# An output projection with seven products in place of eight, and the scheduler that was changed with it

## The chip, the cores and the metric

The kernel runs on all 8 cores of one Trainium2 chip. Each core computes one eighth of the tokens. The metric is the device time of the slowest core, in microseconds (us). Before the change it was 1244.42 us (median of the 3 executions, 1244.34 to 1245.89).

Each execution lists, for every core, its span and the mean clock that TensorE was granted, as a share of full speed. An execution is called slow when one die (cores 0 to 3, or 4 to 7) is over 1% longer than the other at a lower clock, or when its time is over 1.5% above the fastest of the same kernel. The rule has a gap that matters below: when two cores of each die are at a lower clock, the dies agree with each other, and the execution counts as fast unless a quicker one of the same kernel stands beside it.

In the profile PE is TensorE, PEld its weight loads, DVE VectorE, ACT ScalarE, POOL GpSimd, SP the engine that issues most transfers. A name before "<-" is what an instruction writes.

## The reference

Four sequences of 8192 tokens, 1024 wide. What the change touches is the output projection of the mixer, `w_out`, 1024 x 1024. A second part of the block, the squared-ReLU MLP, comes after it and takes over half of the time.

```python
def reference(x, ...):
    h = rmsnorm(x, norm1_g[l])
    p = jnp.einsum('bsd,de->bse', h, w_in[l])          # B, C, x~ | u, v
    ...
    y_a = b_gate * causal_depthwise_conv(c_gate * xc, conv_w[l])
    y_b = u * spatial_gating(layernorm(v, ...), gmlp_ws[l], gmlp_bs[l])
    y = jnp.concatenate([rmsnorm(y_a, out_norm_conv_g[l]),
                         rmsnorm(y_b, out_norm_gmlp_g[l])], axis=-1)
    x = x + jnp.einsum('bse,ed->bsd', y, w_out[l])     # <- the output projection
    h2 = rmsnorm(x, norm2_g[l])
    a = jax.nn.relu(jnp.einsum('bsd,df->bsf', h2, w_up[l]))
    x = x + jnp.einsum('bsf,fd->bsd', a * a, w_down[l])
    return rmsnorm(x, final_g)
```

## The kernel before

A core works on 8 tiles of 512 tokens (`MT = 512`, `NMT = 8`). The mixer goes through the tiles one after the other, until about 440 us. Then the MLP works on pairs of tiles (groups `g`). The MLP already uses a seven-product form (Strassen-Winograd) of its two large products: each operand is cut in four quarters, three sums of quarters are added to it (`[7, 4, ...]` buffers), and seven products of quarters replace eight.

The output projection is plain. Each of 8 output chunks is a sum of 8 matmuls of 128x128 weights on 512 columns:

```python
def out_proj(m):
    b = X[(m + 1) % 3]
    for dc in range(8):
        bank = bank8()
        for e0 in (0, 4):
            pe(bank, [(bank[:, :], WO[:, e_, dc * 128:(dc + 1) * 128], YN[:, e_, :], e_ == 0, e_ == 7)
                      for e_ in range(e0, e0 + 4)], YN.keys(e0, 4) + WO.keys(0, 8))
        tt(b[:, dc, :], bank[:, :], b[:, dc, :], ALU.add, bank.keys() + b.keys(dc), b.keys(dc))
        ...                                    # stores of x1, two chunks at a time
    rs = RS[nxt("rs", 3)]
    rstd(rs[:, :], stats(b, X1Q, 8, ONESD), MT, rs.keys())
    dma("sp", rs_d[m], rs[:, :], rs.keys(), [("rsd", m)], ("rss", m % 2), 4 * 128 * MT)
```

The last statement stores each tile's reciprocal deviations (`RS`) in memory, as `rs_s`. The MLP loads them again, with the stored x1, to make its input `H2` (this is `h2_part`; the table goes to `RSL`, the rows to `XS`):

```python
def h2_part(g, h):
    m, rs = 2 * g + h, RSL[h]
    dma("pool", rs[:, :], rs_d[m], [("rsd", m)], rs.keys(), ("rsl", h), 4 * 128 * MT, margin=4.0)
    for j in range(4):
        xs = XS[nxt("xs", 2)]
        ...
        dma("pool", xs[:, :, :], src, [("x1", m, j)], xs.keys(0, 2), ...)
        for k in (2 * j, 2 * j + 1):
            q = ((3, 2), (4, 1))[k // 4][h]
            stt(H2[:, q, k % 4, :], xs[:, k % 2, :], pcol(G2, k), rs[:, :], ALU.mult, ALU.mult, ...)
```

Buffers have fixed places in the core's memory. Mixer buffers and MLP buffers lie on top of each other, and a write to a place waits for the last reads of whatever lay there: `keys` gives a buffer's kilobytes, and the dependency tracking goes by them. The places that matter (KB, from `o`):

```python
VH = ar.buf("VH", (o + 98) * KB, [4, MT], F16)                                   # mixer
RS = [ar.buf(f"RS{i}", (o + 190 + 2 * i) * KB, [MT], F32) for i in range(3)]     # both
WO = ar.buf("WO", (o + 166) * KB, [8, 1024], F16)                                # mixer
YN = ar.buf("YN", (o + 182) * KB, [8, MT], F16)                                  # mixer
SN = [ar.buf(f"SN{i}", (o + a) * KB, [3, MT], F32) for i, a in enumerate((98, 104, 182))]   # MLP
RSL = [ar.buf(f"RSL{i}", (o + 196 + 2 * i) * KB, [MT], F32) for i in range(2)]   # MLP
```

The order of the instructions on each engine isn't that of the program text. A list scheduler (`S.schedule`) simulates the five engines, picks an order, improves it by some rounds that go backward from the end, and fixes it when the kernel is built.

Of the kernel before, what the change touches and what calls it, by code (L numbers as in the profile page):

```python
# [17 lines left out]
MT = 512  # L18
# [4 lines left out]
HW = 32  # L23
KB = 1024

ENGS = ("pe", "act", "dve", "pool", "sp")

# [35 lines left out]
def real(x):  # L63
    return x.ap() if isinstance(x, Late) else x


class Sched:
# [44 lines left out]
    def schedule(self, phys, rounds=8):  # L112


        base = [(op, op.deps) for op in self.ops]
        best = None
        for _ in range(rounds + 1):
            for op, deps in base:
                op.deps = deps
                for b in op.banks:  # L120
                    b.left = len(b.ops)
            order = self.place([op for op, _ in base], phys)
            est = max(o.finish for o in order)
            if best is None or est < best[0]:
                best = (est, order, [(o, o.deps) for o in order],
                        [(o.opens, o.opens.phys) for o in order if o.opens is not None],
                        {o: (o.start, o.finish) for o in order})
            self.push(order, est)
        self.est_total, self.ops = best[:2]
        for o, deps in best[2]:  # L130
            o.deps = deps
            o.start, o.finish = best[4][o]
        for b, p in best[3]:
            b.phys = p
        self.by_eng = {e: [o for o in self.ops if o.eng == e] for e in ENGS}

    def push(self, order, est, lat=0.12, dma_lat=2.0, dma_rate=290e3):
# [13 lines left out]
        def dur(o):  # L151
            return o.dur if o.dma_key is None else o.occ + o.nbytes / dma_rate + dma_lat + 2 * o.margin
        while True:
# [12 lines left out]
            if o.dma_key is not None:  # L166
                dma_free = min(dma_free, o.late - dma_lat - 2 * o.margin) - o.nbytes / dma_rate
                end = min(end, dma_free)
# [9 lines left out]
    def place(self, ops, phys, lat=0.12, dma_lat=2.0, dma_rate=290e3):  # L178
# [13 lines left out]
        dma_free = 0.0  # L192
        cold = 3.4
        order = []
        while True:
            best = None
            for e in ENGS:
# [5 lines left out]
                def ready_at(o):  # L203
                    return o.ready_t if o.opens is None else max(o.ready_t, soon)
# [10 lines left out]
            if op.opens is not None:  # L215
                f = min(free, key=lambda f: f[1])
                free.remove(f)
                op.opens.phys = f[0]
                op.deps = op.deps + f[2]
# [10 lines left out]
            if op.dma_key is not None:  # L230
                dma_free = max(dma_free, st + op.occ) + op.nbytes / dma_rate
                op.finish = dma_free + dma_lat + op.margin
            else:
                op.finish = st + op.dur - op.occ + occ
# [11 lines left out]
        assert len(order) == len(ops)  # L246
# [73 lines left out]
def build_program():  # L320
# [23 lines left out]
    with es:  # L344
# [23 lines left out]
        SQ = [ar.buf(f"SQ{i}", (o + 68 + 4 * i) * KB, [4, MT], BF16) for i in range(2)]  # L368
        HT = [ar.buf("HT0", (o + 126) * KB, [8, MT], F16), ar.buf("HT1", (o + 76) * KB, [8, MT], F16)]
        PREP = [ar.buf(f"PREP{i}", (o + 84 + 7 * i) * KB, [7, 4, 128], F16) for i in range(2)]  # L370
        VH = ar.buf("VH", (o + 98) * KB, [4, MT], F16)
        CT = [ar.buf(f"CT{i}", (o + 102 + 2 * i) * KB, [MT], F32) for i in range(2)]
        T2 = [ar.buf(f"T2{i}", (o + 106 + 2 * i) * KB, [MT], F32) for i in range(2)]
        X = [ar.buf(f"X{i}", (o + a) * KB, [8, MT], F32) for i, a in enumerate((134, 110, 150))]
        WO = ar.buf("WO", (o + 166) * KB, [8, 1024], F16)
        YN = ar.buf("YN", (o + 182) * KB, [8, MT], F16)
        RS = [ar.buf(f"RS{i}", (o + 190 + 2 * i) * KB, [MT], F32) for i in range(3)]
        XQ = [ar.buf("XQ0", (o + 126) * KB, [8, MT], BF16), ar.buf("XQ1", (o + 76) * KB, [8, MT], BF16)]
        X1Q = ar.buf("X1Q", (o + 182) * KB, [8, MT], BF16)
# [8 lines left out]
        RSL = [ar.buf(f"RSL{i}", (o + 196 + 2 * i) * KB, [MT], F32) for i in range(2)]  # L388
# [7 lines left out]
        HQ = [ar.buf("HQ0", (o + 106) * KB, [8, HW], BF16), ar.buf("HQ1", (o + 108) * KB, [8, HW], F16)]  # L396
        SQH, HH = HQ[0][:, :, :], HQ[1][:, :, :]
        WSB = [ar.buf(f"WSB{i}", (o + 84 + 2 * i) * KB, [MT], F32) for i in range(3)]
# [30 lines left out]
        def act(out, in_, func, reads, writes, n=MT, **kw):  # L429
            aps = sum(1 for v in kw.values() if not isinstance(v, (int, float)))  # L430
            S.add("act", lambda e: e.activation(out=out, in_=real(in_), func=func, **kw), reads=reads, writes=writes,  # L431
                  occ=(n / 1.2 + 200 + 70 * aps) / 1000, banks=[in_.bank] if isinstance(in_, Late) else [])

        def dve(fn, reads, writes, n=MT, rate=1, src=None):
            S.add("dve", fn, reads=reads, writes=writes, occ=(n / rate + 151) / 960,
                  banks=[src.bank] if isinstance(src, Late) else [])
# [71 lines left out]
        def stage0_norm(m, bank, step=4):  # L508
            rs = RS[nxt("rs", 3)]
# [38 lines left out]
        def stage_conv(m, c):  # L548
# [7 lines left out]
            ct = CT[nxt("ct", 2)]  # L556
            act(ct[:, :], bC[:, :], AF.Identity, bC.keys(), ct.keys())
            tt(Z[:, c, 128:640], bX[:, :], ct[:, :], ALU.mult, bX.keys() + ct.keys(), Z.keys(c))
# [7 lines left out]
        def stage_su(m, c):  # L566
# [7 lines left out]
            t2 = T2[nxt("t2", 2)]  # L574
            bias_b = BIAS[:, c, :].unsqueeze(1).broadcast_to([128, 4, 128])
            stt(t2[:, :].rearrange("p (t i) -> p t i", t=4), bS[:, :].rearrange("p (t i) -> p t i", t=4),
                pcol(GLN, c), bias_b, ALU.mult, ALU.add, bS.keys() + [("BIAS",)] + CONST, t2.keys())
            tt(YB[:, c, :], bU[:, :], t2[:, :], ALU.mult, bU.keys() + t2.keys(), YB.keys(c))

        def y_norm(src, q, ebase):  # L580
            rs = RS[nxt("rs", 3)]
            rstd(rs[:, :], stats(src, q, 4, ONESE), MT, rs.keys())
            for c in (0, 2):
                tt(YN[:, ebase + c:ebase + c + 2, :], src[:, c:c + 2, :],
                   rs[:, :].unsqueeze(1).broadcast_to([128, 2, MT]), ALU.mult, src.keys(c, 2) + rs.keys(),
                   YN.keys(ebase + c, 2), n=2 * MT)

        def out_proj(m):
            b = X[(m + 1) % 3]
            for dc in range(8):  # L590
                bank = bank8()
                for e0 in (0, 4):
                    pe(bank, [(bank[:, :], WO[:, e_, dc * 128:(dc + 1) * 128], YN[:, e_, :], e_ == 0, e_ == 7)
                              for e_ in range(e0, e0 + 4)], YN.keys(e0, 4) + WO.keys(0, 8))
                tt(b[:, dc, :], bank[:, :], b[:, dc, :], ALU.add, bank.keys() + b.keys(dc), b.keys(dc))
                if dc % 2:
                    j = dc // 2
                    dst = x1_d[m, :, 2 * MT * j:2 * MT * (j + 1)].rearrange("p (k t) -> p k t", k=2)
                    dma("sp", dst, b[:, 2 * j:2 * j + 2, :], b.keys(2 * j, 2), [("x1", m, j)], ("xs", (m + 1) % 3, j),
                        4 * 128 * 2 * MT)  # L600
            rs = RS[nxt("rs", 3)]
            rstd(rs[:, :], stats(b, X1Q, 8, ONESD), MT, rs.keys())
            dma("sp", rs_d[m], rs[:, :], rs.keys(), [("rsd", m)], ("rss", m % 2), 4 * 128 * MT)

        def combine(p, dst, src, dkeys, reads, margin):
# [4 lines left out]
            tt(p[:, 4, :, :], p[:, 3, :, :], p[:, 2, :, :], ALU.add, p.keys(2, 2), p.keys(4), rate=2)  # L610
            tt(p[:, 3:6:2, :, :], p[:, 0:1, :, :].broadcast_to([128, 2, 4, 128]), p[:, 3:5, :, :], ALU.subtract,
               p.keys(0) + p.keys(3, 2), p.keys(3) + p.keys(5), n=1024, rate=2)
            tt(p[:, 6, :, :], p[:, 1, :, :], p[:, 5, :, :], ALU.add, p.keys(1) + p.keys(5), p.keys(6), rate=2)
# [5 lines left out]
        def prep(i, n):  # L619
            combine(PREP[n % 2], ws(i), wup_d if i < 16 else wdn_d, (i, ("pl", n % 2), ("ps", n % 2)), WO.keys(4) if n < 2 else [], 5.0)  # L620

# [9 lines left out]
        def load_w(n):  # L631
            s, i = wslot(), plan[n]
            if n < 32 and 16 <= i < 24:
# [86 lines left out]

        def down_unit(o_, s0, s1):
            bA, bC, bD = banks_acd()

# [11 lines left out]
            d1, d2 = o_, o_ + 4  # L735
            prod(bA, P1, True, False)
            addr(0, d1, bA)
            prod(bD, P2, True, True)
            addr(0, d1, bD)
            prod(bC, P5, True, False)  # L740
            addr(1, d2, bC)
            prod(bA, P6, False, False)
            addr(1, d1, bA)
            prod(bC, P3, False, True)
            addr(1, d1, bC)
            prod(bA, P7, False, False)
            addr(1, d2, bA)
            prod(bA, P4, False, True)
            addr(0, d2, bA)

        def final(g):

            rss = []
            for h in range(2):
                b, rs = R[h], RS[nxt("rs", 3)]
# [99 lines left out]
        for j in range(2):  # L855
            wload(WO[:, 4 * j:4 * j + 4, :], wo_d[j].rearrange("p (k n) -> p k n", k=4), WO.keys(4 * j, 4), ("o", j),
                  2048 * KB)
            gain(lambda k_: WO[:, k_, :], WO, range(4 * j, 4 * j + 4), GCONV, 1024)
# [38 lines left out]
        def prep_some(m):  # L897
            if m >= 1 and pos["prep"] < 24:
                n = pos["prep"]
                prep(n if n < 16 else n + 8, n)  # L900
# [3 lines left out]
        for m in range(NMT):  # L904
# [16 lines left out]
            y_norm(YA, SQ[0], 0)  # L921
            if last:
                h2_part(0, 1)
                h2_sums()
# [144 lines left out]
```

## Time and profile before

| | before |
|---|---|
| time, median | 1244.42 us |
| spans of the 8 cores in the profiled execution | 1235.7 to 1244.9 us |
| granted clock, mean of each core | 0.991 to 0.995 |
| PE busy | 1209.6 us, 97% of the span |
| DVE busy | 893.4 us, 72% |
| output projection on PE | 512 matmuls of 512 columns |

These lines are from the page of the kernel before (core 7, the slowest): the busy times, the granted clock in 40 slices of the span in tenths, the chain of work that ended last, and the group of the output projection's matmuls (busy time, mean ns of one, idle before).

```profile
PE 1209.6 (97%) x5880; PEld 548.5 (44%) x5880; DVE 893.4 (72%) x1377; ACT 530.4 (43%) x905; POOL 86.0 (7%) x146
...
PEclk9899999999999999999999999999999999999998
...
PE 93%; DMA 5%; DVE 1%; issue 0%; SPq 0%; DVEq 0%; POOLq 0%
...
L424 PE MATMUL PS<-YN,WO 128*128 128x512 f16 x512 | 113.8, 379 | 0.0
```

PE is the chain. The mean of 379 ns is the time from a matmul's start to its end in the pipeline. What a matmul costs is the distance between starts. On core 7's PE timeline 368 matmuls of 512 columns start in the 79.43 us from 719.62 to 799.05 us, 215.8 ns apart. (The prediction took 100 us / 465 = 215.05 ns from the last line of the next view. That is a little too low: a window counts every matmul that touches it, one that began before it too.) The view is the windows of core 7, with the busy time of each engine and its instructions, the granted clock, the share of the transfer engines and GB/s.

```profile
core 7: us, PE busy (x) PEld busy (x) DVE busy (x) ACT busy (x) POOL busy (x), PEclk, DMA share, GB/s
...
100.00:400.00 300.00, 300.00 (x1534) 135.22 (x1533) 235.63 (x328) 157.08 (x268) 15.36 (x29) 1.00 0.73 199
400.00:425.00 25.00, 25.00 (x118) 11.27 (x115) 19.58 (x30) 9.56 (x15) 2.13 (x4) 1.00 0.94 305
425.00:450.00 25.00, 25.00 (x141) 11.25 (x140) 22.58 (x31) 13.49 (x22) 1.60 (x3) 1.00 0.55 180
...
660.00:760.00 100.00, 100.00 (x465) 45.31 (x464) 69.04 (x109) 37.29 (x66) 11.29 (x16) 1.00 0.72 243
```

PE has no gap in any of these windows. DVE has some slack in the mixer (235.63 of 300 us), and the least in the stretch from 425 to 450 us, where the mixer turns into the MLP (22.58 of 25). I call that stretch the turn. Why PE doesn't wait there shows in the POOL timeline of core 1, in which GpSimd issues the loads for `H2` (start, duration, what, and in brackets the idle time before and what ended it):

```profile
169.83 0.54 POOL L450 DMA_DIRECT2D RSL_100<-rs_s  x1 [3.02 <-DMA rs_s<-RS_79]
...
407.94 0.53 POOL L450 DMA_DIRECT2D XS_94<-x_s  x1 [11.21 <-DVE H_96 L442]
```

The table of tile 1's deviations (RSL_100) was asked for at 169.83 us, long before it was needed. The second half of `H2` was complete at 425.42 us (DVE timeline), and its sums began at 426.60 us. So PE had MLP matmuls (those that read H_96) to put between the last pieces of the mixer, as its timeline of core 1 shows:

```profile
430.54 1.89 PE L424 MATMUL PS<-H_96,RING_83 128*128 128x512 f16 x8
432.26 1.03 PE L424 MATMUL PS<-H_96,RING_84 128*128 128x512 f16 x4
433.12 1.89 PE L424 MATMUL PS<-H_96,RING_83 128*128 128x512 f16 x8
...
438.31 1.89 PE L424 MATMUL PS<-YN,WO 128*128 128x512 f16 x8
```

### The profile page before, as it was taken

What the parts mean: (1) busy time and instruction counts of PE and PEld (TensorE: products, weight loads), DVE (VectorE), ACT (ScalarE), POOL (GpSimd) and SP (SyncE); (2) the same over time, 40 slices, a digit from 0 to 9 for tenths busy, and PEclk for the clock granted to TensorE, in tenths of its full rate; (3) what the DMA queues carried; (4) which work ended last, traced back from release to release, by engine and by line L of the source; (5) the groups of instructions that cost most, each with busy time, mean ns of one, the idle gap of its engine ahead of it and who ended that gap; (6) DMA issues with size and microseconds to landing.
All of it is one profiled execution on the core that took longest, in us unless ns stands there. A gap on an engine that the chain in (4) does not pass through costs nothing.

```text
span 1244.9 us, 18564 instructions; the slowest of 8 cores (1235.7 to 1244.9 us)
## 1 busy us (share of the span) xinstructions
PE 1209.6 (97%) x5880; PEld 548.5 (44%) x5880; DVE 893.4 (72%) x1377; ACT 530.4 (43%) x905; POOL 86.0 (7%) x146
## 2 busy tenths in 40 slices
PE   5899999999999999999999999999999999999994
PEld 3444444444444444444444444444444444444442
DVE  2778687877878887658759737767846876855746
ACT  4544655536554356026127205317405406503524
POOL 0100000000001011000101200000110000110000
PEclk9899999999999999999999999999999999999998
DMA  8968688596675869975577764576984645985423
GB/s 185 171 148 232 167 228 231 148 245 175 179 220 153 279 213 207 237 266 176 169 260 228 262 212 162 211 237 177 295 272 148 216 165 182 279 271 177 149 90 135
DMA packets 55183, 253.81 MB, mean 204 GB/s; under 512 B 6192, under 2 KB 6320, under 8 KB 54832
## 3 DMA queue, kind: packets, MB, share of 16 engines
q1 hardware_dynamic: 35152, 180.27, 42.8%
q0 software_dynamic: 19936, 72.36, 25.3%
q8 instruction: 49, 0.80, 0.3%
q14 instruction: 46, 0.38, 0.1%
HBM read 211.71 MB, written 65.01 MB: 222 GB/s over the span
## 4 chain that ended last, share of the span: by engine, by line
PE 93%; DMA 5%; DVE 1%; issue 0%; SPq 0%; DVEq 0%; POOLq 0%
PE PS L424 93%; DMA WSB_109<-bsf 2%; DMA X_74<-xT 1%; DMA X_73<-xT 1%; DMA WV<-wv 1%; DMA WCXB_53<-wcxb 1%; DVE RA L439 0%; DVE RB L439 0%; SPq L450 0%; DVE WU L446 0%; DVEq L344 0%; DVE FSQ_102 L439 0%; DVE FSQ_101 L439 0%; DVE Z L439 0%; DVEq L284 0%
## 5 line engine op out<-in xcount | busy, mean ns | idle before, releaser
L439 DVE TENSOR_TENSOR RB<-PS,RB 128x512 f32<-128x512 f32 x128 | 87.4, 690 | 91.4 <-PE PS L424 88.9
L424 PE MATMUL PS<-YN,WO 128*128 128x512 f16 x512 | 113.8, 379 | 0.0
L439 DVE TENSOR_TENSOR RA<-PS,RA 128x512 f32<-128x512 f32 x96 | 66.1, 690 | 60.6 <-PE PS L424 59.2
L439 DVE TENSOR_TENSOR A_89<-A_89 128x512 bf16<-128x512 bf16 (+1 forms) x192 | 94.5, 508 | 8.2 <-ACT A_89 L431 3.6
L431 ACT ACTIVATE SN_92<-PS 128x512 f32<-128x512 f32 x63 | 37.4, 595 | 106.5 <-PE PS L424 104.7
L424 PEld LDWEIGHTS PS<-YN,WO 128*128 128x128 f16 x512 | 50.1, 98 | 60.4
L424 PE MATMUL PS<-A_89,RING_83 128*128 128x512 bf16 x308 | 76.1, 379 | 0.0
L424 PE MATMUL PS<-A_89,RING_85 128*128 128x512 bf16 x308 | 76.1, 379 | 0.0
L424 PE MATMUL PS<-A_89,RING_86 128*128 128x512 bf16 x308 | 75.8, 379 | 0.0
L424 PE MATMUL PS<-A_89,RING_84 128*128 128x512 bf16 x308 | 75.5, 379 | 0.0
L424 PE MATMUL PS<-H_96,RING_87 128*128 128x512 f16 x308 | 75.1, 379 | 0.0
L424 PE MATMUL PS<-H_96,RING_83 128*128 128x512 f16 x308 | 74.5, 379 | 0.0
L424 PE MATMUL PS<-H_96,RING_88 128*128 128x512 f16 x308 | 74.3, 379 | 0.0
L424 PE MATMUL PS<-H_96,RING_84 128*128 128x512 f16 x308 | 74.3, 379 | 0.0
L431 ACT ACTIVATE SN_90<-PS 128x512 f32<-128x512 f32 x66 | 39.2, 595 | 76.7 <-PE PS L424 75.6
L424 PE MATMUL PS<-A_89,RING_88 128*128 128x512 bf16 x280 | 69.4, 379 | 0.0
L424 PE MATMUL PS<-A_89,RING_87 128*128 128x512 bf16 x280 | 69.1, 379 | 0.0
L431 ACT ACTIVATE SN_93<-PS 128x512 f32<-128x512 f32 x64 | 38.2, 596 | 71.8 <-PE PS L424 71.3
L424 PE MATMUL PS<-H_96,RING_85 128*128 128x512 f16 x280 | 67.9, 379 | 0.0
L424 PE MATMUL PS<-H_96,RING_86 128*128 128x512 f16 x280 | 67.4, 379 | 0.0
L431 ACT ACTIVATE SN_91<-PS 128x512 f32<-128x512 f32 x63 | 37.5, 595 | 70.1 <-PE PS L424 68.0
L439 DVE TENSOR_TENSOR SN_92<-PS,SN_92 128x512 f32<-128x512 f32 x63 | 43.4, 690 | 27.4 <-PE PS L424 22.7
(231 smaller groups left out, 2029.2 us busy)
## 6 DMA issues: line engine op xcount, KB each, us to landing
RING_83<-ws_s SPq DMA_DIRECT2D x21, 896.0 KB, 6.0
RING_84<-ws_s SPq DMA_DIRECT2D x21, 896.0 KB, 6.4
RING_87<-ws_s SPq DMA_DIRECT2D x20, 896.0 KB, 5.3
RING_88<-ws_s SPq DMA_DIRECT2D x20, 896.0 KB, 6.2
RING_85<-ws_s SPq DMA_DIRECT2D x19, 896.0 KB, 6.0
RING_86<-ws_s SPq DMA_DIRECT2D x19, 896.0 KB, 6.3
ws_s<-PREP_65 SPq DMA_DIRECT2D x12, 896.0 KB, 6.3
ws_s<-PREP_66 SPq DMA_DIRECT2D x12, 896.0 KB, 5.6
```

Of the source, the lines that this page charges most:

```text
L424: ins = e.matmul(real(o_), lhsT=l, rhs=r, start=st, stop=sp, skip_group_check=True)
L431: S.add("act", lambda e: e.activation(out=out, in_=real(in_), func=func, **kw), reads=reads, writes=writes, occ=(n / 1.2 + 200 + 70 * aps) ...
L439: dve(lambda e: e.tensor_tensor(out=out, in0=real(in0), in1=in1, op=op), reads, writes, n, rate, in0)
```

## The change

The intent is to give the output projection the same seven-product form, so that PE has an eighth less to do there, and to schedule better. The diff has these parts:

1. `WO` and `YN` become quarters with sums, `[7, 4, ...]`. The columns of a tile are cut in two token halves, so the matmuls have 256 columns, and there are 896 of them instead of 512. DVE makes the sums of `YN` for each tile and those of `WO` once, and adds 14 PSUM results per tile instead of 8.
2. `WO` grows from 16 to 28 KB and `YN` from 8 to 14 KB, so the buffers are placed anew.
3. The scheduler models two transfer queues that share a rate, tries 60 disturbed orders, and picks the one that is best on average over 6 draws of late transfers. Its costs of ACT and DVE instructions are new too.
4. In the last tile, the second half of `H2` comes after the loop of `stage_su` in the program text, not before it.
5. Small changes go with these: two temporaries (`CT`, `T2`) are gone and their results are made in place in `Z` and `YB`, other weights of the down product are combined during the mixer, and the scheduler holds back some PSUM banks.

```diff
-        VH = ar.buf("VH", (o + 98) * KB, [4, MT], F16)
+        YN = ar.buf("YN", (o + 68) * KB, [7, 4, MT // 2], F16)
+        RS1 = [ar.buf(f"RS1{i}", (o + 104 + 2 * i) * KB, [MT], F32) for i in range(3)]
-        WO = ar.buf("WO", (o + 166) * KB, [8, 1024], F16)
-        YN = ar.buf("YN", (o + 182) * KB, [8, MT], F16)
-        RS = [ar.buf(f"RS{i}", (o + 190 + 2 * i) * KB, [MT], F32) for i in range(3)]
+        WO = ar.buf("WO", (o + 166) * KB, [7, 4, MT], F16)
+        VH = ar.buf("VH", (o + 194) * KB, [4, MT], F16)
...
-        RSL = [ar.buf(f"RSL{i}", (o + 196 + 2 * i) * KB, [MT], F32) for i in range(2)]
+        RS2 = [ar.buf(f"RS2{i}", (o + 190 + 2 * i) * KB, [MT], F32) for i in range(3)]
+        RSL = [ar.buf(f"RSL{i}", (o + 198 - 2 * i) * KB, [MT], F32) for i in range(2)]
...
         def out_proj(m):
-            for dc in range(8):
-                ...
+            x = X[(m + 1) % 3]
+            half = MT // 2
+            for dc in (0, 2):
+                def prod(bank, p, first, last):
+                    a, b = p
+                    pe(bank, [(bank[:, half * u:half * (u + 1)], WO[:, a, k, (dc + u) * 128:(dc + u + 1) * 128],
+                               YN[:, b, k, :], first and u == 0 and k == 0, last and k == 3)
+                              for u in range(2) for k in range(4)],
+                       YN.keys(b) + WO.keys(a))
+                ...
+                winograd(prod, add, dc)        # 7 products, 7 adds
+            rs = RS1[nxt("rs", 3)]
+            rstd(rs[:, :], stats(x, X1Q, 8, ONESD), MT, rs.keys())
             dma("sp", rs_d[m], rs[:, :], rs.keys(), [("rsd", m)], ("rss", m % 2), 4 * 128 * MT)
...
-            y_norm(YA, SQ[0], 0)
+            y_norm(YA, SQ[0], (3, 2))
             if last:
-                h2_part(0, 1)
-                h2_sums()
                 refill(4)
             for c in range(4):
                 stage_su(m, c)
+            if last:
+                h2_part(0, 1)
+                h2_sums()
+            y_norm(YB, SQ[1], (4, 1))
+            tsum(lambda i, j, d: YN[:, i:j:d, :, :], lambda j: YN.keys(j), 2 * MT)
...
-    def schedule(self, phys, rounds=8):
+    def schedule(self, phys, rounds=8, tries=60):
+        draws = [{op: rnd.choice((0.0, 0.0, 0.0, 1.0)) * rnd.uniform(1.0, 8.0) * (not op.fixed) for op in dmas} for _ in range(6)]
+        ...                                    # 60 disturbed orders, the best mean over the draws is kept
```

## The prediction

> **What bounds it now.** The TensorE matmul stream. The chain of waits is 93% PE, one unbroken run from 68.7 to 1227.0 us. In the windows from 100 to 1200 us PE is busy without a gap at granted clock 1.00; 100 us of the MLP hold 465 matmuls of 512 columns, 215.05 ns each. Outside that run lie 68.7 us of start (about 50 us PE busy, the rest waiting for loads) and 18 us of tail. DVE is busy 37.5 to 42 of every 50 us in the mixer windows (100 to 450 us): second, not binding.
>
> **Removed.** By the groups, the output projection is 512 matmuls of 512 columns: 512 x 0.215 = 110.1 us, all inside the unbroken run.
>
> **Added.** 7/8 of the columns, as 896 matmuls of 256 columns. The profile has none of that width. Estimate: [...] the start's burst of fifty-two 128-wide ones takes 55 ns each, each with its weight load hidden. So a 256-wide one should take 108.5 ns: 97.2 us. [...] Saving on PE: **12.9 us**.
>
> **DVE pays.** Per tile 14 instead of 8 PSUM adds (six more at 0.605 us, the start-to-start distance in the DVE timeline; their 690 ns "mean" overlaps) and about 2.3 us of half-precision sums of YN: +6 us in a tile of about 49.5 us. DVE goes from about 39 of 49.5 to about 45 of 48 us, some 93%. DVE frees the PSUM banks, so small PE stalls may appear in the mixer; I allow 1.5 us. Once, WO needs sums too (about 4.5 us of DVE near 85 to 95 us); other PE work covers them. ACT (about 26 of 50 us) has room. The MLP, over half of the time, keeps its instructions.
>
> **Start and tail.** PE loses about 19 us to waits and some 3 us to a low clock before 68.7 us, waiting for transfers (DMA share 0.82 to 1.03 up to 60 us), which the change does not shorten, only splits and reorders. One thing looks worse: in the new DVE order the gain multiplications of the fourth conv weight's (WCXB) second half and of WU's second half stand behind the BIAS add that waits for the bsf table, which landed at 66 us. If it lands as late again, PE runs dry earlier. A better model of two queues may win elsewhere. Net allowance +1.5 us, uncertain by 4. Tail unchanged within 1 us. The late-transfer part of the scheduler can win nothing in the middle: PE has no gap there.
>
> **Sum.** 1244.4 - 12.9 + 1.5 + 1.5 - 0.5 = about **1234 us** (0.8% faster), 8 in 10 between 1226.5 and 1241.5. Faster by over 2%: 0.04; within 2%: 0.94; slower by over 2%: 0.02.
>
> **What would show it.** Right: the YN,WO group becomes 896 matmuls of 128x256 spaced 108.5 ns in the timeline; DVE busy rises by 45 to 50 us, to near 940, above 44 of 50 in mixer windows; MLP windows still 465 matmuls per 100 us; the unbroken PE run about 1146 us long. Stall step: PE busy under 50 of 50 in mixer windows, released by DVE adds. Start step: where the unbroken run begins, with a PE wait on WCXB or WU gains.
>
> **What would make it wrong.** Spacing well above 108.5 ns (weight loads not hidden at 256 columns); DVE saturating in the mixer and stalling PE by more than 5 us; a start 5 us or more longer or shorter through the new order; a late transfer meeting the fixed orders; a lower granted clock.

The sum came to 1244.4 - 12.9 + 1.5 + 1.5 - 0.5 = 1234.0 us. The 108.5 ns was the estimate. The measured numbers give nearly the same: a straight line from 55 ns at 128 columns (the 52 matmuls of the start) to 215.05 ns at 512 gives 108.35 ns at 256, 97.1 us for 896 of them, and a saving of 13.0 us in place of 12.9.

## The result, and the profile after

| | before | changed |
|---|---|---|
| time, median of 4 | 1244.38 us (1243.37 to 1245.89) | 1286.27 us |
| all executions | 1244.42, 1244.34, 1245.89, 1243.37 | 1287.64, 1485.55, 1284.06, 1284.9 |
| ratio of the fast executions | | 1.0332 (1.0302 to 1.0363) |

A ratio is the mean time of one kernel's fast executions over that of the other's fast executions of the same rounds, so it isn't quite the ratio of the medians. The interval is the 95% one. The changed kernel is 3.3% slower, not 0.8% faster. In the fast executions of the changed kernel behind this ratio a pair of cores on each die was at 0.960 to 0.966, so it isn't a comparison at equal clock; the controls below are.

The lines of the page that answer to those shown of before (core 4, the slowest; its clock wasn't that of core 7 before, so the sums can't be compared directly):

```profile
PE 1230.3 (96%) x6264; PEld 594.6 (46%) x6264; DVE 942.6 (73%) x1460; ACT 531.2 (41%) x905; POOL 87.7 (7%) x148
...
PEclk9999999999999997888889999999999999999997
...
PE 91%; DMA 4%; DVE 2%; issue 1%; ACT 1%; SPq 0%; DVEq 0%; ACTq 0%
...
L496 PE MATMUL PS<-YN,WO 128*128 128x256 f16 x896 | 107.2, 276 | 5.4 <-DVE YN L512 3.1
```

The PEclk row drops to 7 and 8 tenths in slices 16 to 21 of 40. The list of cores of the same execution, with span and mean granted clock, shows on whom:

```profile
core 0: 1245.7 us, clock 0.990
core 1: 1236.9 us, clock 0.991
core 2: 1283.2 us, clock 0.963
core 3: 1279.7 us, clock 0.960
core 4: 1286.1 us, clock 0.960
core 5: 1280.7 us, clock 0.964
core 6: 1241.1 us, clock 0.990
core 7: 1246.1 us, clock 0.986
```

So there are two effects. Cores 2 to 5, at a lowered clock, took 38 to 50 us longer than in the profile before. But the cores that kept their clock (0, 1, 6, 7) didn't gain anything either: core 1 took 1236.9 us, against 1237.7 us before.

**Core 1: where the saving went.** Its PE timeline first shows that the matmuls have the predicted cost, 40 of them from 91.52 to 95.89 us, that is 109.2 ns each. Then, at the turn, it shows four waits that the kernel before had not:

```profile
91.52 4.53 PE L496 MATMUL PS<-YN,WO 128*128 128x256 f16 x40
95.89 0.59 PE L496 MATMUL PS<-HT_66,WCXB_52 128*128 128x512 f16 x2
...
398.79 0.41 PE L496 MATMUL PS<-WST,VH 128*64 128x128 f16 x8
...
429.81 5.40 PE L496 MATMUL PS<-YN,WO 128*128 128x256 f16 x48 [2.43 <-DVE YN L512]
435.87 1.91 PE L496 MATMUL PS<-YN,WO 128*128 128x256 f16 x16 [0.66 <-DVE X_76 L512]
439.49 2.78 PE L496 MATMUL PS<-YN,WO 128*128 128x256 f16 x24 [1.72 <-DVE X_76 L512]
444.75 1.02 PE L496 MATMUL PS<-H_92,RING_79 128*128 128x512 f16 x4 [2.47 <-DVE H_92 L512]
```

They sum to 7.28 us. Every core has three or four of these waits, 5.15 to 7.28 us in sum. The POOL timeline of core 1 shows what was late:

```profile
399.75 0.54 POOL L523 DMA_DIRECT2D RSL_99<-rs_s  x1 [1.43 <-ACT Z L503]
416.21 0.53 POOL L523 DMA_DIRECT2D XS_90<-x_s  x1 [15.92 <-DVE H_92 L515]
...
420.02 0.53 POOL L523 DMA_DIRECT2D XS_91<-x_s  x1
```

RSL_99 is the table that was asked for at 169.83 us before. Now it is asked for at 399.75 us, right after the last matmul that reads VH (398.79 us, the third line of the PE rows), on which it lies. The bracket names an ACT write of Z, the releaser that came last by the profile, but Z isn't on that place; the load leaves 0.55 us after the end of those matmuls (398.79 + 0.41 us), and did so on every core that was looked at. It took 12.4 us to land. The multiplications that make `H2` wait for it, they free the XS buffers late, and the last loads leave at 416 and 420 us. The second half of `H2` was complete at 441.2 us (before: 425.4). So PE had no MLP matmuls to fill the time in which DVE finishes the mixer, and stood still.

The windows of core 1 count it: PE was busy 17.73 of 25 us at the turn, with DVE at 22.81 of 25, much as before (22.03 in the same window of this core).

```profile
100.00:400.00 300.00, 299.33 (x1888) 167.65 (x1887) 275.14 (x392) 162.76 (x274) 15.60 (x30) 1.00 0.74 199
...
425.00:450.00 25.00, 17.73 (x124) 12.17 (x123) 22.81 (x31) 8.40 (x13) 3.04 (x5) 0.93 0.66 210
...
500.00:550.00 50.00, 50.00 (x234) 22.64 (x232) 19.32 (x28) 5.66 (x10) 0.55 (x1) 1.00 0.41 133
```

A further cost comes after some of these waits: a clock of half speed for a while. On core 4 the same 48 matmuls took 6.93 us where they took 5.40 us on core 1, and the granted clock was 0.50 from 431.2 to 434.4 us. The 0.93 in the second line above comes from such a stretch on core 1: after the last of its waits the granted clock was 0.70 in the mean from 444.7 to 448 us. Over 418 to 510 us, in the control below, the waits of PE are 13.0 us in the mean over 8 cores, and the half clock takes about 3.4 us more. Before, it was 0.3 us of waits and none.

**Core 4: a second wait, then the clock.** Seven of the 8 cores have another wait between 480 and 500 us, of 2.4 to 11.85 us. These are rows of core 4's timelines of SP, ACT and PE, in that order:

```profile
468.47 1.40 SPq L523 DMA_DIRECT2D rs_s<-RS_72  x1
```

```profile
496.85 0.60 ACT L503 ACTIVATE SN_87<-PS 128x512 f32<-128x512 f32 x1 [12.87 <-DMA rs_s<-RS_72]
```

```profile
497.59 1.87 PE L496 MATMUL PS<-H_92,RING_83 128*128 128x512 f16 x4 [11.85 <-ACT SN_87 L503]
```

The last tile's deviations are stored from RS_72, and the store landed 28.3 us after its issue (the three before it from that buffer took 8.1 to 11.9 us on this core), among loads of weights with the transfer engines at 0.95 of their time (the window from 485 to 490 us). The first write to that part of SN_87 that lies on RS_72 in the new places waited for it (other parts had been written at 470.94 and 471.80 us), and PE waited for a free bank.

Then the clock. The windows of core 4:

```profile
450.00:500.00 50.00, 38.09 (x171) 16.98 (x170) 28.48 (x46) 21.68 (x38) 5.59 (x8) 0.88 0.87 233
500.00:550.00 50.00, 50.00 (x188) 20.56 (x187) 21.90 (x34) 7.40 (x13) 0.00 (x0) 0.80 0.31 106
550.00:660.00 110.00, 110.00 (x421) 45.56 (x420) 69.17 (x112) 33.09 (x57) 7.98 (x15) 0.81 0.63 167
660.00:760.00 100.00, 100.00 (x463) 45.24 (x462) 78.31 (x125) 40.81 (x67) 12.87 (x19) 1.00 0.83 279
```

The granted clock was 0.50 from 490 to 502 us, during and after the wait. From about 503 to 662 us PE ran at 0.81, and did 421 matmuls in 110 us where it did 511 before (cores 3 and 7). The two cores of a pair went down and came back together: 159.5 us on both cores 4 and 5, 162.8 us on both cores 2 and 3. That is about 160 x (1 - 0.81) = 30 us of work. Then, under the same load, the clock returned to full speed: 1.00, with 463 matmuls in the 100 us from 660 us on core 4. Core 1 kept 1.00 from 500 to 760 us.

So two cores of each die were lowered and the other two were not (mean clock 0.960 to 0.964 on cores 2 to 5, 0.986 to 0.991 on the others), although PE had been busy for 409 to 422 of the 430 us from 70 to 500 us on all 8.

**A ledger.** To compare runs I use a lag: a moment t of the PE timeline, minus the columns of all matmuls that started by then, at 2.4 columns per ns (2400 per us). This is the rate at full clock by the spacings above: 256 columns more cost 215.8 - 109.2 = 106.6 ns, and 256 / 106.6 = 2.40. The mean over 8 cores, in us (the expectations below worked from sums over windows, which count some matmuls twice and give lags lower by up to 9 us):

| profiled execution | at 100 us | 420 | 510 | 1200 |
|---|---|---|---|---|
| before | 24.1 | 28.8 | 30.6 | 41.1 |
| changed, result run (pairs lowered) | 25.9 | 31.7 | 51.5 | 76.4 |
| changed, first control below (none lowered) | 25.9 | 31.7 | 50.2 | 61.7 |

About 1% of the records of two cores in each profile are missing, which raises their lag a little. The changed kernel has 32768 columns less per core (896 x 256 against 512 x 512), 13.65 us. For an execution without lowered pairs: -13.65 (columns), +1.8 (start, 25.9 - 24.1), +1.1 (mixer from 100 to 420 us, 5.8 against 4.7), +16.7 (420 to 510 us, 18.5 against 1.8), +1.0 (MLP, 11.5 against 10.5). The sum is +7.0 us; the mean span of the 8 cores rose by 6.6 us (1240.0 to 1246.6), which agrees. So the stretch from 420 to 510 us alone eats more than the saving.

### The profile page after: what moved, and what is told of

It is laid out like the page before. It is cut to its first block, busy times and chain, and to the rows that moved or that the text cites. A ratio compares the mean times of both kernels' runs of the same rounds, so it can differ in the third digit from the quotient of the medians.

```text
span 1286.1 us, 19491 instructions; the slowest of 8 cores (1236.9 to 1286.1 us)
## 1 busy us (share of the span) xinstructions
PE 1230.3 (96%) x6264; PEld 594.6 (46%) x6264; DVE 942.6 (73%) x1460; ACT 531.2 (41%) x905; POOL 87.7 (7%) x148
## 3 DMA queue, kind: packets, MB, share of 16 engines
q0 software_dynamic: 21760, 72.36, 25.9%
## 4 chain that ended last, share of the span: by engine, by line
PE 91%; DMA 4%; DVE 2%; issue 1%; ACT 1%; SPq 0%; DVEq 0%; ACTq 0%
PE PS L496 91%; DMA rs_s<-RS_72 2%; DMA X_76<-xT 1%; DMA X_75<-xT 1%; DVE RA L512 0%; DVE RB L512 0%; DVE YN L512 0%; DVE X_76 L512 0%; SPq L523 0%; DVE H_92 L512 0%; ACT XQ_68 L503 0%; ACT RS_73 L503 0%; ACT RS_71 L503 0%; ACT DUMP_56 L503 0%; DVE WCXB_54 L519 0%
## 5 line engine op out<-in xcount | busy, mean ns | idle before, releaser
L496 PE MATMUL PS<-YN,WO 128*128 128x256 f16 x896 | 107.2, 276 | 5.4 <-DVE YN L512 3.1
L496 PEld LDWEIGHTS PS<-YN,WO 128*128 128x128 f16 x896 | 88.2, 99 | 26.7 <-issue 7.4
L503 ACT ACTIVATE SN_87<-PS 128x512 f32<-128x512 f32 x63 | 37.4, 595 | 134.5 <-PE PS L496 121.5
L496 PE MATMUL PS<-H_92,RING_83 128*128 128x512 f16 x308 | 78.2, 393 | 11.9 <-ACT SN_87 L503 11.9
L496 PE MATMUL PS<-A_85,RING_81 128*128 128x512 bf16 x308 | 80.9, 395 | 0.0
L496 PE MATMUL PS<-A_85,RING_82 128*128 128x512 bf16 x308 | 80.8, 394 | 0.0
L496 PE MATMUL PS<-A_85,RING_80 128*128 128x512 bf16 x308 | 79.3, 389 | 0.0
L496 PE MATMUL PS<-A_85,RING_79 128*128 128x512 bf16 x308 | 79.3, 389 | 0.0
L496 PE MATMUL PS<-H_92,RING_79 128*128 128x512 f16 x308 | 76.7, 385 | 2.5 <-DVE H_92 L512 2.5
L496 PE MATMUL PS<-H_92,RING_80 128*128 128x512 f16 x308 | 78.1, 396 | 0.0
L496 PE MATMUL PS<-H_92,RING_84 128*128 128x512 f16 x308 | 76.7, 389 | 0.0
L503 ACT ACTIVATE SN_86<-PS 128x512 f32<-128x512 f32 x66 | 39.3, 596 | 87.3 <-PE PS L496 87.1
L496 PE MATMUL PS<-A_85,RING_83 128*128 128x512 bf16 x280 | 72.2, 388 | 0.0
L496 PE MATMUL PS<-A_85,RING_84 128*128 128x512 bf16 x280 | 71.7, 387 | 0.0
L503 ACT ACTIVATE SN_88<-PS 128x512 f32<-128x512 f32 x63 | 37.1, 594 | 82.8 <-PE PS L496 82.8
L496 PE MATMUL PS<-H_92,RING_81 128*128 128x512 f16 x280 | 70.5, 385 | 0.0
L496 PE MATMUL PS<-H_92,RING_82 128*128 128x512 f16 x280 | 70.4, 388 | 0.0
L512 DVE TENSOR_TENSOR SN_87<-PS,SN_87 128x512 f32<-128x512 f32 x63 | 43.1, 688 | 36.4 <-PE PS L496 18.2
L512 DVE TENSOR_TENSOR SN_88<-PS,SN_88 128x512 f32<-128x512 f32 x63 | 43.1, 688 | 27.4 <-PE PS L496 19.0
```

The source lines that it names most:

```text
L496: ins = e.matmul(real(o_), lhsT=l, rhs=r, start=st, stop=sp, skip_group_check=True)
L503: S.add("act", lambda e: e.activation(out=out, in_=real(in_), func=func, **kw), reads=reads, writes=writes, occ=(n / 1.2 + 70 + 70 * aps) ...
L512: dve(lambda e: e.tensor_tensor(out=out, in0=real(in0), in1=in1, op=op), reads, writes, n, rate, in0)
```

## The experiments

Theories at this point:

- The turn: the waits come from the new places (RSL on VH, SN on RS). Rivals: the new scheduler's order makes them; or VectorE simply has too much to do in the last tile.
- The clock: the waits of PE just before bring it (A); or it comes with this instruction stream whatever its waits, or with chip and moment.

Letters in the expectations below are those of the time they were written; in the second call, C is "the place of RSL" and D "VectorE is crowded"; in the calls after it, A is "the wait brings the lowered clock", B "the instruction stream", C "chip and moment". In kernels made for experiments the profile leaves out the buffer numbers of names (H for H_92, SN for SN_87).

### First call, four kernels on chip 1: before 1245.52 us, median of 7

**e0_after_again: the changed kernel, unedited.** A control on another chip.

> The changed kernel itself, again, perhaps on another chip. If the slowdown belongs to the program (a wait for the store of the last tile's rstd, then a lowered clock), it comes back here: about 1280 to 1290 us, a PE wait of 5 to 12 us near 490 us for ACT SN, and on some pairs of cores a granted clock near 0.81 for about 165 us after it. If it was a mood of that chip, this comes at about 1240 to 1250 us with a clock near 0.99 on all cores.

Measured: 1258.67, 1250.51, 1251.65 us fast, ratio 1.0063 (1.0031 to 1.0095), and one slow one, 1483.3 us, with cores 2 and 3 at 0.964 and 0.961 beside die 1 at 0.81 to 0.82. So without the lowered clock the changed kernel is 0.6% slower than before, and the 33 us more of the result run's fast executions (41 against 8 us above before) go with the clock. The waits at the turn were there on all 8 cores, the one on the rs_s store too (0.9 to 9.7 us).

**e1_rs_moved: only the last tile's deviations elsewhere.** The order of every engine is the changed kernel's (it was frozen, and compared instruction by instruction). The dependencies were worked out anew for the new place, where nothing of the first MLP steps lies.

```diff
-            rs = RS1[nxt("rs", 3)]
-            rstd(rs[:, :], stats(x, X1Q, 8, ONESD), MT, rs.keys())
-            dma("sp", rs_d[m], rs[:, :], ...)
+            at = RS2[2] if m + 1 == NMT else rs        # applied after scheduling, order kept
+            rstd(at[:, :], stats(x, X1Q, 8, ONESD), MT, rs.keys())
+            dma("sp", rs_d[m], at[:, :], ...)
```

> The changed kernel with the order of every engine frozen as it was; only the last tile's rstd is kept in a buffer that no SN tile overlaps, so that the first SN write does not wait for its store. Theory A (that wait makes PE idle for 9 to 12 us, and the idle stretch is what lowers the clock of a pair of cores afterwards): the wait is gone, no window below 0.97 clock between 500 and 680 us, all cores 1228 to 1240 us, time about 1236 to 1240 us. Rival B (the clock is lowered by the heavier load of the new mixer, or by the 7 us of waits at 426 to 447 us, and the store wait is a bystander): the store wait is gone, but some cores still show 0.81 for over 100 us, and the time stays above 1265 us.

Measured: 1250.38, 1243.22, 1254.82, 1250.9 us, ratio 1.0033 (0.9997 to 1.0069). The wait for SN is gone from all cores, which shows its cause. The mean lag at 510 us fell from 50.2 to 43.8 us. The time expected (1236 to 1240 us) was missed. Some cores wait instead for a weight load that used to hide behind that wait, core 3 for instance:

```profile
497.72 2.72 PE L524 MATMUL PS<-A,RING 128*128 128x512 bf16 x6 [4.37 <-DMA RING<-ws_s]
```

The waits of 7 us at the turn stay. No execution had a lowered pair.

**e2_before_stalls: the kernel before, made to wait.** Its order is frozen, and 23, 13 and 43 activations on a table that is no longer used are put before three points of the MLP, so that ScalarE holds up PE there.

```diff
+        for u, n in [(4, 23), (28, 13), (44, 43)]:
+            at, new = ups[u][1], []
+            for _ in range(n):
+                act(BIAS[:, :, :], BIAS[:, :, :], AF.Identity, [], [])
+                ...
+            S.insert(at, new)
```

> The kernel before, its order frozen, with ACT held up by dummy activations at three places of the MLP, about 14, 8 and 26 us long (near 505, 790 and 980 us), so that PE runs dry for an estimated 11, 5 and 23 us. Theory A (a PE idle stretch of some 9 us and more lowers the clock of a pair of cores afterwards, whatever the kernel): after the first and the third place some cores show about 0.81 for 100 us and more, after the second hardly any; the time is 1244 + about 39 us of waits + up to 30 us for each lowered stretch. Rival B (the lowered clock belongs to the new mixer): clock 1.00 again within 10 us of every place on all cores, time about 1244 + 35 to 45 us.

Measured: 1300.18, 1296.63, 1295.52 us, ratio 1.0404 (1.0383 to 1.0425), one slow. The windows of core 3 (the first of the three stalls lies in the first line below; it was 14.38 us long):

```profile
450.00:500.00 50.00, 35.62 (x154) 15.41 (x153) 23.67 (x37) 34.31 (x56) 7.34 (x11) 0.83 0.70 180
500.00:550.00 50.00, 50.00 (x234) 22.68 (x232) 36.19 (x67) 8.41 (x15) 2.64 (x5) 1.00 0.82 214
550.00:660.00 110.00, 110.00 (x512) 49.83 (x511) 76.35 (x116) 38.10 (x64) 5.31 (x10) 1.00 0.65 207
```

The clock is back at 1.00 in the window after. In this profile all 8 cores stood still at the first point for 14.4 us, at the second for 3.6 us and at the third for 25.4 us, and in none of the four executions was a pair lowered. So stands of 14.4 and 25.4 us at these places didn't bring the lowered clock of pairs in these four executions.

**e6_new_math_old_order: the new arithmetic and places with the scheduler and the costs of before.**

```diff
-    def schedule(self, phys, rounds=8, tries=60):      # and Queues, replay, the new costs of ACT and DVE
+    def schedule(self, phys, rounds=8):                # all of these as in the kernel before
```

> The seven-product output projection and its buffer places, but with the scheduler and instruction costs of the kernel before. If the new scheduler's order is what lost the time at the turn to the MLP (its waits of 7 us at 426 to 447 us on every core), this has smaller waits there. If it is the arithmetic (DVE crowded by YN sums and extra adds) or the places of buffers, waits of 7 us or more stay, and so does a wait of SN for the rstd store (its buffer is the same). I expect the waits to stay, 1245 to 1290 us, and the start to be no better than before.

Measured: 1254.08, 1260.75, 1255.12, 1254.46 us, ratio 1.0083 (1.006 to 1.0107). The lag grows by 19.4 us from 420 to 510 us (32.0 to 51.4), as with the new scheduler (18.5), in another pattern of waits; a wait on the rs_s store is among them. So waits of this size don't need the new scheduler. They come with the arithmetic, the places and the small changes of part 5. Against what was expected, its start is better than the changed kernel's (22.2 against 25.9 us at 100 us); its mixer is worse (9.8 against 5.8 us).

### Second call, four kernels on chip 7: before 1244.97 us, median of 11, three of them slow

**e0b_after_third: the changed kernel, five rounds.**

> The changed kernel once more, to count how often a pair of cores shows a clock near 0.96 for the whole run (0.81 for some 165 us), which 3 of 4 executions showed in the result and, on the next chip, only one execution out of four. If it belongs to a chip or a moment, here it is either nearly always there (time about 1280 to 1290 us) or nearly never (1250 to 1258 us); if it belongs to the program, about half of the executions have it.

Measured: 1251.79, 1259.98, 1252.72 us fast, ratio 1.0078 (1.004 to 1.0117). Four more at 1279.76 to 1282.1 us, each with one pair of cores at 0.963 to 0.965, and one at 1366.32 us with a pair and a whole die lowered. So the changed kernel has two states on one chip, some 27 us apart (mean 1281.3 against 1254.8 us).

**e7_rsl_moved: RSL for the second half of the first group elsewhere.** One new buffer, and the scheduler runs again.

```diff
+        RSL0B = ar.buf("RSL0B", (o + 138) * KB, [MT], F32)
-            m, rs = 2 * g + h, RSL[h]
+            m, rs = 2 * g + h, RSL0B if (g, h) == (0, 1) else RSL[h]
```

> Only the buffer for the second rstd of the first MLP pair (RSL, second) is moved off the bytes of VH, to a part of H2 that is not yet written; the rest is as in the changed kernel, scheduled anew. Theory C (the waits of 7 us at 426 to 447 us come from this overlap: the load could start only after the last read of VH, landed 14 us later, so H2's second half was late and PE had no MLP products to fill the wait for YN): the waits at the turn fall from about 7 us to under 2.5 us on every core; the wait of SN for the rstd store (5 to 12 us) is still there; time 4 to 8 us below the changed kernel's in the same call. Rival D (DVE is crowded by the YN sums and the extra adds in the last tile): the waits stay at 5 us or more.

Measured: 1245.08, 1245.02, 1244.87 us, ratio 0.9999 (0.9963 to 1.0035), one slow with die 0 lowered. This is 9.8 us below the changed kernel's fast mean of the call (1254.8 us), where 4 to 8 us were expected. The four waits of 7 us became one of 0.23 or 0.24 us on every core, and the lag grows by 6.7 us from 420 to 510 us. Core 4 for instance:

```profile
437.07 1.02 PE L497 MATMUL PS<-H,RING 128*128 128x512 f16 x4 [0.24 <-DVE SN L513]
```

The wait on the rs_s store stays on 6 of the 8 cores (3 to 5 us). So the place of RSL is a cause of the waits at the turn, with a caution: the scheduler ran again, and the order of the instructions differs from the changed kernel's almost from the start. No run moved RSL alone in a frozen order.

**e8_both_moved: both places.** The RSL edit of e7, and the last tile's deviations in RS2[2], with the scheduler run again.

```diff
+        RSL0B = ar.buf("RSL0B", (o + 138) * KB, [MT], F32)
-            rs = RS1[nxt("rs", 3)]
+            rs = RS1[nxt("rs", 3)] if m + 1 < NMT else RS2[2]
-            m, rs = 2 * g + h, RSL[h]
+            m, rs = 2 * g + h, RSL0B if (g, h) == (0, 1) else RSL[h]
```

> Both buffers moved: RSL's second off VH, and the last tile's rstd off the SN tiles. If theories A (store wait) and C (late H2) hold, no wait over 2.5 us is left at the turn except for weights of the ring that land late, the lag gained between 420 and 510 us falls from about 17.6 us to under 6 us, and the time is 1234 to 1241 us: below the kernel before by 4 to 11 us. If waits for ring weights take the place of those removed, it is 1240 to 1248 us.

Measured: 1232.35, 1236.7, 1238.08, 1237.81, 1238.68 us, ratio 0.9933 (0.9907 to 0.9959), and one slow one with die 0 lowered. This is faster than both kernels, by 0.7% than the kernel before. The clock of the slow one was 0.955 and 0.959 on cores 2 and 3, and 0.937 and 0.938 on cores 0 and 1. The POOL timeline of core 1 shows the table asked for at 357.73 us, and the XS loads at 408 and 409 us again; the windows show the turn:

```profile
357.73 0.54 POOL L524 DMA_DIRECT2D RSL0B<-rs_s  x1 [6.28 <-ACT Z L504]
...
408.15 0.53 POOL L524 DMA_DIRECT2D XS<-x_s  x1 [12.82 <-DVE H L516]
```

```profile
425.00:450.00 25.00, 24.61 (x157) 15.05 (x156) 25.00 (x33) 12.84 (x22) 0.53 (x1) 1.00 0.62 219
450.00:500.00 50.00, 50.00 (x245) 23.85 (x244) 40.08 (x64) 27.36 (x46) 5.68 (x8) 1.00 0.82 250
```

PE is busy 24.61 of 25 us at the turn, and DVE all 25: the slack there is used up. The lag grows by 1.7 us from 420 to 510 us (31.2 to 32.9), against 1.8 before and 18.5 in the control.

**e9_last_plain: the last tile's projection in eight products.** The places stay as in the changed kernel. A lighter last tile for VectorE: no sums of YN, 8 adds instead of 14; one subtraction gives the plain quarter of WO back.

```diff
+            for dc in range(8 if m + 1 == NMT else 0):
+                ...                                    # plain products of quarters
-            for dc in (0, 2):
+            for dc in (0, 2) if m + 1 < NMT else ():
...
-            tsum(lambda i, j, d: YN[:, i:j:d, :, :], lambda j: YN.keys(j), 2 * MT)
+            if last:
+                tt(WO[:, 3, :, :], WO[:, 0, :, :], WO[:, 3, :, :], ALU.subtract, ...)
+            else:
+                tsum(lambda i, j, d: YN[:, i:j:d, :, :], lambda j: YN.keys(j), 2 * MT)
```

> The changed kernel with the last tile's output projection in plain eight-product form (same halves and banks; no YN sums, 8 adds instead of 14, about 6 us less DVE work at the turn, 1.8 us more PE work). Rival D (DVE crowded at the turn): the waits of 7 us at 426 to 447 us fall to under 3 us. Theory C (H2's second half late by its load): they stay at 5 us or more, and the rstd store wait stays.

Measured: 1245.32, 1241.94, 1243.12, 1239.04 us, ratio 0.9978 (0.995 to 1.0007). Of the waits at the turn, one or more remained on 6 cores, 0.29 to 2.98 us by core, and none on the other two, although RSL still lay on VH, which I had not expected from the theory of places alone. On core 1 the table was asked for as late as in the changed kernel, and the second half of `H2` was complete at 438.06 us (changed kernel: 441.2), so a late `H2` alone doesn't make waits of 7 us:

```profile
398.92 0.54 POOL L523 DMA_DIRECT2D RSL<-rs_s  x1 [3.07 <-ACT Z L503]
...
436.65 1.41 DVE L515 SCALAR_TENSOR_TENSOR H<-XS,PRM,RSL 128x512 f16<-128x512 f32 x2
```

So the rival holds as well: as far as e7 and e9 tell, it takes the late `H2` and a full DVE together, and either a lighter last tile or an earlier `H2` removes most of these waits. The wait on the rs_s store stays (0.6 to 4.5 us), and the lag grows by 7.6 us from 420 to 510 us. Here too the scheduler ran again.

### Third call, four kernels on chip 2: inconclusive

I wanted the lowered pairs: the control again (e0c), with the rs_s wait removed (e1b), the kernel before with stalls (e2b), and e1 with 18 dummy activations before that very SN instruction (e11).

```diff
+        for _ in range(18):                            # e11, on top of e1
+            act(BIAS[:, :, :], BIAS[:, :, :], AF.Identity, [], [])
```

> Positive control for the lowered clock: so far 9 of 16 executions of the changed kernel had at least one pair of cores (0 and 1, 2 and 3, and so on) at a mean clock near 0.964, and none of 22 of the kernel before. Expected here: 2 to 5 of 6 executions. If it is 0, this chip says nothing about the other three runs.

> Frozen order, only the store wait taken away. Theory A (PE idle for about 10 us behind the store wait is what lowers a pair's clock): no execution with a pair near 0.964; the fast ones near 1250 us. Rival B (the new mixer's load lowers it): as often as in the control of this call.

> The kernel before with PE idle for 14, 4 and 25 us. Theory A: pairs whose mean clock is 0.02 to 0.03 (or twice that) below the 0.975 of their neighbours in some executions, as often as in the control. Rival B: none, as on the earlier chip.

> The changed kernel in its frozen order with the store wait taken away, but ACT held up at the very same instruction for about 11 us by dummy activations, on every core alike. Theory A (an idle PE is enough): pairs near 0.96 come back as often as in the control, and the time is about 1255 us without and 1290 us with them. Theory A2 (it takes the store wait itself, or cores idle for unequal times): no lowered pair, about 1255 to 1260 us in every fast execution.

On this chip every kernel had a mean clock of about 0.92 (die 0) and 0.94 (die 1) in most executions, and lower on one die in a few, the kernel before too. The mean is a mixture: core 1 of e0c (1317.0 us at a mean of 0.929 in the profiled execution) went back and forth between 1.00 and 0.81, in stretches of 15.0 us at 0.81 (30 of them, at the same times on core 0). The times were slow throughout: medians 1335.42 us before, 1326.3 (e0c), 1323.7 (e1b), 1387.51 (e2b), 1339.73 (e11). The control showed no lowered pair, so the call says nothing of them. I draw no ratio from it.

### Fourth call, four kernels on chip 12: inconclusive for the same reason

> The changed kernel again, as the control. On a chip at full clock: fast runs 1250 to 1260 us, and about half of its executions with one pair of cores at a mean granted clock of 0.96 to 0.97 and 1280 us. If none shows a pair, this call can't tell the theories apart (C gains). If the chip is at a lower clock throughout, it says nothing.

> Same order, only the last tile's reciprocal deviations kept elsewhere, so that its SN write doesn't wait for the rs_s store. A (the wait brings the lowered pair): no execution with a lowered pair, fast runs 1245 to 1252 us. B (the instruction stream): about half of the executions with a lowered pair, as in the control. C: a rate that has nothing to do with the control's.

> As the run with the rstd moved, with 18 dummy activations just before that SN write, which hold ScalarE for about 10 us there on every core. A: lowered pairs come back in about half of the executions or more, on pairs in which both cores stand still; fast runs 1250 to 1260 us. B: the same rate as with the rstd moved, whatever that is.

> Both places moved, no waits at the turn. A: no lowered pair, 1236 to 1240 us, 0.5 to 0.9 per cent below the kernel before. B: lowered pairs in about half of the executions, near 1270 us.

Again a chip with lowered mean clocks throughout, 0.90 and 0.93: medians 1364.06 us before, 1358.28 (e0d), 1358.56 (e1c), 1371.22 (e11b), 1354.32 (e8c). The control showed no pair. The kernel with both places moved had the lowest median here too.

### Fifth call, two kernels on chip 7: before 1245.4 us, median of 11

> The changed kernel, the control. On a chip at full clock about half of its executions with one pair of cores at a mean granted clock of 0.96 to 0.97 and 1280 us, the others 1250 to 1260 us. Without a pair, or on a chip at a lower clock throughout, this call can't tell the theories apart.

Measured: fast 1256.5, 1255.46, 1246.96, 1248.54 us, ratio 1.0053 (1.0021 to 1.0086). Two executions with lowered pairs, 1282.86 us (cores 0/1 and 4/5 at 0.963 to 0.967) and 1284.19 us (4/5 at 0.964 and 0.961). The profiled execution, without a lowered pair, has waits of 9.79 and 9.83 us for SN on cores 4 and 5. These are as long as those of the pairs that were lowered in the result run (8.98 to 11.85 us). So the length of this wait alone doesn't decide.

> Same order, only the wait of the last tile's SN write on the rs_s store taken away. A: no execution with a lowered pair, 1245 to 1252 us. B: about half of the executions with a lowered pair, near 1280 us, as in the control.

Measured: 1252.03, 1241.92, 1255.67, 1250.33, 1242.25, 1244.14 us, ratio 1.0013 (0.9974 to 1.0052), no lowered pair in six.

The kernel **before** had an execution of 1276.16 us with cores 4 and 5 at 0.968 and 0.969 and all others at 0.991 and up. So this state isn't the changed kernel's own.

### The count of lowered pairs

Executions on chips at full clock. I count one when both cores of a pair (0/1, 2/3, 4/5, 6/7) had a mean clock of 0.960 to 0.969. The slow execution of e8 falls just outside (0.955 and 0.959, with the whole die lowered) and isn't counted.

| kernel | executions | with a lowered pair |
|---|---|---|
| before | 33 | 1 |
| changed | 22 | 11 |
| changed, rs_s wait removed (e1) | 10 | 0 |
| changed, RSL moved (e7), rs_s wait there, 3 to 5 us on 6 cores | 4 | 0 |
| both moved (e8) | 6 | 0 |
| last tile plain (e9) | 4 | 0 |
| new arithmetic, old order (e6) | 4 | 0 |
| before with stalls (e2) | 4 | 0 |

That the changed kernel has this state far more often than before is plain from the counts. That removing the rs_s wait ends it is likely, not shown: on the same chips in the same calls it is 3 of 10 against 0 of 10, which equal rates would give about 1 time in 10. On chip 7 in the second call the changed kernel had it in 5 of 8 executions, and e7, e8 and e9 together in 0 of 14, which equal rates would give about 1 time in 470; but these three differ from it in order and places, and e7 and e9 keep a shorter wait on the rs_s store, so what ended it there isn't told. What brings the state stays open. The idle time alone did not where it was tried or seen (e2, 14.4 and 25.4 us on all 8 cores; the fifth call's profile, 9.79 and 9.83 us on cores 4 and 5). How the pauses of the cores and the return of load combine was not tried: the two runs made for it (e11, e11b) fell on chips at a lower clock.

## Why the prediction was wrong

**The saving on PE: right.** Predicted 896 matmuls at 108.5 ns. They took 109.2 ns, so 896 x 0.1092 = 97.8 us in place of 512 x 0.2158 = 110.5 us, and the saving was 12.7 us where 12.9 was predicted. Both figures of the prediction are a little low, since 215.05 ns was: a window counts every matmul that touches it, one that began before it too. Weight loads stayed hidden: there is one for each of the 896 matmuls, 99 ns in the mean on core 4, and the spacing was 109.2 ns with them.

**DVE pays: right in the amount.** DVE rose to 942.6 us, predicted near 940. By the starts in core 1's DVE timeline a PSUM add took 0.60 us, the sums of YN 2.33 us a tile and those of WO 4.47 us, where 0.605, 2.3 and 4.5 were predicted. In the mixer from 100 to 400 us DVE was busy 275.14 of 300 us, and PE lost 0.67 us there on core 1 and, from 100 to 420 us, 1.1 us more than before by the ledger. The 1.5 us that I allowed fit the steady mixer.

**Start: right.** Predicted +1.5 us, measured +1.8 us of lag at 100 us. A short wait for WCXB's gain (0.19 us) is in the PE timeline at 60 us, as told.

**The step that failed: "DVE frees the PSUM banks, so small PE stalls may appear in the mixer; I allow 1.5 us."** I took the stalls for an average matter of DVE's busy share. They came in one place, from 420 to 510 us, and cost 16.7 us more than before (waits, and about 3 us of half clock after them). Two overlaps of the new buffer places are behind them: RSL on VH, together with a DVE that is full there (the waits of 7 us at the turn; e7 brought them to 0.24 us), and SN on RS (the wait of up to 12 us; gone in e1 and e8). The diff showed both overlaps. I read the sizes of the new buffers and not what lay under them. The turn is also the place where before had the least slack on DVE, 22.58 of 25 us, which I had in the profile and averaged away; e9 shows that a lighter last tile removes most of the waits there as well. "Other PE work covers them", which I wrote of the sums of WO at the start, was true there; at the turn the work that would have covered the waits is what came late.

**A lower granted clock was named and not priced.** The last line of the prediction lists it. It was 0.81 for some 160 us on cores 2 to 5 of the profiled execution, and executions that have it are some 26 to 33 us longer. No term of the sum stood for it. This is most of the 3.3%: the fast executions without it are 0.5% to 0.8% slower. Its cause stays open.

**"The late-transfer part of the scheduler can win nothing in the middle": not contradicted.** e6 has the old scheduler and nearly the same growth of lag from 420 to 510 us (19.4 against 18.5 us). "A late transfer meeting the fixed orders" was in the list of what could go wrong, and it is a fair name for one part of what happened: the 256 KB store of rs_s landed after 28.3 us.

**With the overlaps gone, the sum holds.** e8 took 1237.94 us, 3.9 us from the predicted 1234.0 and inside its range. So the terms that I had were of the right size, and the missing one, apart from the clock, was the stretch from 420 to 510 us.

Shown: SN on RS causes its wait (e1, where only that place changed and the order was frozen); waits of this size come without the new scheduler too (e6). Shown with the order made anew, so that a part of the order isn't excluded: with RSL off VH the waits at the turn go (e7, e8), and a lighter DVE in the last tile removes most of them too (e9). Argued only: that the lowered clock of pairs is tied to the rs_s wait.

## What to carry to other kernels

When a change makes buffers larger, list for every moved buffer what now lies on its place, and for each such pair who must finish before whom; look first at the turns between stages, where a load leaves early only if its place is free (the one of RSL left at 169.83 us before and at 399.75 us after). Read the slack of the engine that gets more work in the window where it has least, not as an average over a stage. And look at the clock of each core before explaining a time: here one half of the chip (0.960 to 0.964) told a different story from the other (0.986 to 0.991).
